# A hybrid attention block with a mixture of experts: how the overflow tables are stored, and which engine clears the row buffers

## The chip, the cores and the metric

The kernel runs on one core of one Trainium2 chip. The metric is the device time of one launch in microseconds; before the change the median of three runs is 1189.38 us (1186.39 to 1190.62).

## The reference, cut to what matters

One transformer block over 512 tokens of width 1024: three mixing branches (dilated attention, a gated recurrence, attention to a memory), gates, an output product, a layer norm, a two-level mixture of experts, a second layer norm. The change lies in the experts' part. Each token picks one of 4 groups and 2 of its 8 experts, so 1024 token-expert pairs go to 32 experts; each expert is two products (1024 to 256, twice) and one (256 to 1024):

```python
glog = (ht @ w_rg) + b_rg;  gsel = argmax(glog)
elog = ((ht @ w_re) + b_re).reshape(T, 4, 8);  top_v, top_i = top_k(elog[arange(T), gsel], 2)
weights = softmax(top_v) * gprob[gsel]
def expert_block(xb, e):
    return (silu(xb @ w_gate[e]) * (xb @ w_up[e])) @ w_down[e]
y[token] += weight * expert_block(row of token, e)          # for both picks
x = layer_norm(ALPHA * x + y)
```

## The kernel before, in words

The kernel is one long program without loops on the chip, written in Python loops. Each engine (PE, DVE, ACT, POOL, SP) has its own queue of instructions, which it works off in order; waits between engines are semaphores. The order inside a queue is made by the framework's planner from the order of the source and its own estimates, so neighbours in a queue need not be neighbours in the source.

**Before the experts.** Projections, the three branches and the output product keep PE busy up to about 850 us of the span. `norm_and_route(c)` (L660) does layer norm and routing for each of four classes of 128 tokens: the logits, the two picks (`gi`, `ei`, one-hot `oh`), the rank of each pair within its expert (`cums`, by a product with a triangle, copied by ACT at L695). `gain_and_store(c)` (L698) finishes the rows and stores them to `x1d` in DRAM.

**The experts.** Each expert has a capacity of 64 rows, and two experts make one pass `p` of 128 rows, 16 passes in all (loop at L992). The rows of a pass are `xs`. For passes 0 and 1, `gather` (L756) makes them with one-hot products on PE (L767), whose one-hot matrices `oh0` and `ohg` DVE writes in `picked` (L657). For passes 2 to 15, `fetch` (L750) gathers rows from `x1d` by an indirect DMA of POOL into one of three buffers `xg0` to `xg2`, and PE transposes them (L778). The three buffers are cleared once before the loop (L989), on POOL, as empty slots are not fetched. `gate_up` (L782, matmuls L789) makes the two first products, `silu2` the activation (L193, L194), L1010 transposes, L1023 makes the last product, and ACT and DVE scale it by the slot's weight into `y` (L1029, L1031). POOL scatters `y` by an indirect DMA to `yd` (L1037) for passes 0 to 13.

**The weights.** The experts' weights are 192 tiles of 512 KB, 12 in each pass (four `gate_up` tiles and two `down` tiles for each of two experts). `expert_raw` (L615) loads them on SP's queue (L114) into a ring of 33 buffers: a tile can be loaded when PE has used the tile 33 before it. The `gate_up` tiles of a pass come free as its L789 goes on, its `down` tiles in its L1023. After the 192 tiles SP loads `yd` back (L1046), and the second layer norm follows.

**The tables.** After `gate_up(0)` is issued, `tables` (L818) makes, for each slot, the token (`tok`, `gidx`) and the weight (`wsl`), by `slot_tables` (L793): one-hot matrices and a product (L805) into columns 0 to 15 of these [128, 24] tables. `overflow_tables` (L860) does the same for pairs beyond an expert's capacity: columns 16 to 23, eight columns of 128 slots, stored to DRAM as `ovg_d` (tokens) and `ovw_d` (weights) of 1024 numbers each (L899, L900, on POOL's queue), with a list of experts `ove_d` (L911). In DRAM slot `s` of column `p` lies at `p*128 + s`, so a column runs down the partitions on chip but is contiguous in DRAM. `overflow` (L913) reads the three in a loop at the end of the program, once for each block of 64 such rows; the profiled execution has no instruction of the loop's body (L918 on).

The scratch tiles of both functions are pieces of one buffer of the tag `yp` (L996), which has two buffers; `y` of the passes rotates through the same two (L1013), so `y` of pass 1 takes the buffer in which the scratch tiles were.

Of the kernel before, what the change touches and what calls it, by code (L numbers as in the profile page):

```python
# [13 lines left out]
I32 = mybir.dt.int32  # L14
# [22 lines left out]
def build(tc, ins, out, dbg=None):  # L37
# [5 lines left out]
    def T(pool, shape, dt=F32, tag=None, **kw):  # L43
        cnt[0] += 1
        tag = tag or f"u{cnt[0]}"
        return pool.tile(list(shape), dt, name=f"{tag}_{cnt[0]}", tag=tag, **kw)
# [23 lines left out]
    V, S, TE, G = nc.vector, nc.scalar, nc.tensor, nc.gpsimd  # L70
# [4 lines left out]
    def bank(tag, w=512, dt=F32):  # L75
        t = T(ps, [128, 512], dt, tag=tag)
        return t[:, :w] if w != 512 else t

    ident = T(cp, [128, 128], tag="ident")
# [9 lines left out]
    ovg_d = T(mdram, [1024, 1], I32, tag="ovg")  # L89
    ovw_d = T(mdram, [1024, 1], tag="ovw")  # L90
# [177 lines left out]
    with cpool:  # L268
        for h in range(4):
# [12 lines left out]
            o = bank("o")  # L282
            for c in range(4):
                cs = slice(c * 128, (c + 1) * 128)
                sc = bank("sc", 256)
# [4 lines left out]
                p = T(tp, [128, 256], tag="cp")  # L290
# [15 lines left out]
    with tc.tile_pool(name="a0", bufs=2, side="right") as tp:  # L306
# [3 lines left out]
        for j in range(5):  # L310
# [4 lines left out]
            pt = bank("sc")  # L315
# [238 lines left out]
    gidx = T(sp, [128, NPAIR], I32, tag="gidx")  # L554
    tok = T(sp, [128, NPAIR], tag="tok")
    wsl = T(sp, [128, NPAIR], tag="wsl")
    yidx = T(sp, [128, PDR], I32, tag="yidx")
    ovi = T(sp, [1, 17], I32, tag="ovi")
    lp = es.enter_context(tc.tile_pool(name="late", bufs=1))
# [13 lines left out]
    i512, i128, i64, i32, i16 = (kc[:, 0:n] for n in (512, 128, 64, 32, 16))  # L573
# [182 lines left out]
    def gather(p):  # L756

        xs = T(mp, [128, 8, 128], tag="xs")
        pts = []
        if p < PEG:  # L760
            oh_ = oh0 if p == 0 else T(mp, [128, 4, 128], tag="ohg", bufs=1)
            pts = [bank("o" if p == 0 else "tr") for _ in range(2)]
            for c in range(4):
                if p > 0:
                    picked(c, p, oh_)
                for k in range(8):
                    TE.matmul(pts[k // 4][:, k % 4 * 128:(k % 4 + 1) * 128], x1[:, c, k * 128:(k + 1) * 128],  # L767
                              oh_[:, c, :], start=c == 0 and k % 4 == 0, stop=c == 3 and k % 4 == 3)
        else:
            xg = xgs[p % AHEAD]  # L770
        for j in range(2):
            if p < PEG:
                pt = pts[j]
            else:
                pt = bank("tr")
                for k in range(4):
                    kk = j * 4 + k
                    TE.transpose(pt[:, k * 128:(k + 1) * 128], xg[:, kk * 128:(kk + 1) * 128], ident)  # L778
            (S.copy if j == 0 else V.tensor_copy)(xs[:, j * 4:(j + 1) * 4, :].rearrange("p k r -> p (k r)"), pt)
        return xs  # L780
# [12 lines left out]
    def slot_tables(lp, row, where, w3, lo, n):  # L793

        sA = T(lp, [128, 8, 128], BF, tag="sA")
        V.tensor_tensor(sA, i128[:, None, :].to_broadcast([128, 8, 128]), row.to_broadcast([128, 8, 128]),
                        op=OP.is_equal)
        sB = T(lp, [128, 8, 5, n], BF, tag="sB")
        V.tensor_scalar(sB[:, :, 0, :], where, pcol, None, op0=OP.mult)
        V.tensor_tensor(sB[:, :, 1, :], where, bval[:, :, None].to_broadcast([128, 8, n]), op=OP.mult)  # L800
        for i in range(3):
            V.tensor_tensor(sB[:, :, 2 + i, :], where, w3[:, i, :, None].to_broadcast([128, 8, n]), op=OP.mult)
        acc = bank("sc", 5 * n)
        for a in range(8):
            TE.matmul(acc, sA[:, a, :], sB[:, a, :, :].rearrange("p a b -> p (a b)"), start=a == 0, stop=a == 7)  # L805
        t = T(lp, [128, 5, n], tag="st")
        V.tensor_copy(t.rearrange("p a b -> p (a b)"), acc)
        g = slice(lo, lo + n)
        V.scalar_tensor_tensor(tok[:, g], t[:, 0, :], BIG, t[:, 1, :], op0=OP.add, op1=OP.add)
        if lo == 0:  # L810
            V.tensor_copy(yidx, tok[:, 0:PDR])
        V.tensor_scalar(t[:, 0, :], tok[:, g], 512.0, -512.0, op0=OP.is_ge, op1=OP.mult)
        V.tensor_tensor(tok[:, g], tok[:, g], t[:, 0, :], op=OP.add)
        V.tensor_copy(gidx[:, g], tok[:, g])
        V.tensor_tensor(wsl[:, g], t[:, 2, :], t[:, 3, :], op=OP.add)
        V.tensor_tensor(wsl[:, g], wsl[:, g], t[:, 4, :], op=OP.add)
# [43 lines left out]
    def overflow_tables(lp):  # L860

        oh8 = oh.rearrange("p c k e -> p (c k) e")
        t32 = T(lp, [128, 8, 32], tag="t32")
        cnt = bank("sc", 32)
        for d in range(4):
            for k in range(2):
                TE.matmul(cnt, oneb, oh[:, d, k, :], start=d == 0 and k == 0, stop=d == 3 and k == 1)
        nb7 = T(lp, [128, 32, 7], tag="nb7")
        V.tensor_tensor(nb7, cnt[:, :, None].to_broadcast([128, 32, 7]),
                        i7[:, None, :].to_broadcast([128, 32, 7]), op=OP.is_gt)  # L870
        nbl = T(lp, [128, 32], tag="nbl")
        V.tensor_reduce(nbl, nb7, axis=AX.X, op=OP.add)
        inc = T(lp, [128, 32], tag="inc")
        V.tensor_tensor_scan(inc, oneb[:, :32], nbl, 0.0, op0=OP.mult, op1=OP.add)
        exc = T(lp, [128, 32], tag="exc")
        V.tensor_tensor(exc, inc, nbl, op=OP.subtract)
        ob = T(lp, [128, 8, 1], tag="ob")
        V.tensor_tensor(t32, oh8, exc[:, None, :].to_broadcast([128, 8, 32]), op=OP.mult)
        V.tensor_reduce(ob, t32, axis=AX.X, op=OP.add)
        t7 = T(lp, [128, 8, 7], tag="t7")  # L880
        V.tensor_tensor(t7, rank8.to_broadcast([128, 8, 7]), i7[:, None, :].to_broadcast([128, 8, 7]), op=OP.is_ge)
        fl = T(lp, [128, 8, 1], tag="fl")
        V.tensor_reduce(fl, t7, axis=AX.X, op=OP.add)
        row = T(lp, [128, 8, 1], tag="row8")
        V.scalar_tensor_tensor(row, fl, -64.0, rank8, op0=OP.mult, op1=OP.add)

        blk = T(lp, [128, 8, 1], tag="blk")
        V.scalar_tensor_tensor(blk, t7[:, :, 0:1], 64.0, ob, op0=OP.mult, op1=OP.add)
        V.scalar_tensor_tensor(blk, fl, -65.0, blk, op0=OP.add, op1=OP.add)
        oh16 = T(lp, [128, 8, 16], tag="oh16")  # L890
        V.tensor_tensor(oh16, i16[:, None, :].to_broadcast([128, 8, 16]), blk.to_broadcast([128, 8, 16]), op=OP.is_equal)
        ohp = oh16.rearrange("p a (b w) -> p a b w", w=2)
        pair = T(lp, [128, 8, 8], tag="pair")
        V.tensor_reduce(pair, ohp, axis=AX.X, op=OP.add)
        par = T(lp, [128, 8, 1], tag="par8")
        V.tensor_reduce(par, ohp[:, :, :, 1], axis=AX.X, op=OP.add)
        V.scalar_tensor_tensor(row, par, 64.0, row, op0=OP.mult, op1=OP.add)
        slot_tables(lp, row, pair, w3, 16, 8)
        G.dma_start(ovg_d.rearrange("(p s) o -> s (p o)", s=128), gidx[:, 16:])  # L899
        G.dma_start(ovw_d.rearrange("(p s) o -> s (p o)", s=128), wsl[:, 16:])  # L900
        z1, z2 = (T(lp, [1, 16, 32], BF, tag=t) for t in ("sA", "t32"))
        ib = i128[0:1, 0:16, None].to_broadcast([1, 16, 32])
        V.tensor_tensor(z1, ib, exc[0:1, None, :].to_broadcast([1, 16, 32]), op=OP.is_ge)
        V.tensor_tensor(z2, ib, inc[0:1, None, :].to_broadcast([1, 16, 32]), op=OP.is_lt)
        V.tensor_tensor(z1, z1, z2, op=OP.mult)
        V.tensor_tensor(z1, z1, i32[0:1, None, :].to_broadcast([1, 16, 32]), op=OP.mult)
        ovf = T(lp, [1, 16], tag="ovf")
        V.tensor_reduce(ovf, z1, axis=AX.X, op=OP.add)
        V.tensor_copy(ovi[:, 0:16], ovf)
        V.tensor_copy(ovi[:, 16:17], inc[0:1, 31:32])  # L910
        G.dma_start(ove_d.rearrange("a o -> o a"), ovi[:, 0:16])  # L911
# [74 lines left out]
    xgs = []  # L986
    for j in range(AHEAD):
        xgs.append(T(mp, [128, 1024], tag=f"xg{j}", bufs=1))
        G.memset(xgs[j], 0.0)  # L989
    xs = gather(0)  # L990
    group = []
    for p in range(16):  # L992
        expert_raw(12 * p + 12 + len(ring))
        gu = gate_up(p, xs)
        if p == 0:
            part = Parts(T(mp, [128, 2048], tag="yp"))  # L996
            tables(part)
            overflow_tables(part)
            for j in range(1, AHEAD + 1):
                fetch(j)  # L1000
# [7 lines left out]
        pt = bank("tr", 256)  # L1008
# [185 lines left out]
```

## Time and profile before

| what | value |
|---|---|
| median of three runs | 1189.38 us |
| profiled execution, its own time | 1191.01 us |
| its span in the trace | 1189.1 us |
| PE busy | 1111.0 us (93%) |
| DVE busy | 504.1 us (42%) |
| ACT busy | 442.9 us (37%) |
| POOL busy | 84.7 us (7%) |
| moved by DMA | 200.91 MB, mean 169 GB/s |

The span is what the trace covers, and the execution's own time is 1.9 us longer. Busy shares are means over stages with different limits: the mean rate of 169 GB/s hides stages with 400 GB/s. Times such as "908" are us from the span's start.

### The profile page before, as it was taken

What the parts mean: (1) busy time and instruction counts of PE and PEld (TensorE: products, weight loads), DVE (VectorE), ACT (ScalarE), POOL (GpSimd) and SP (SyncE); (2) the same over time, 40 slices, a digit from 0 to 9 for tenths busy, and PEclk for the clock granted to TensorE, in tenths of its full rate; (3) what the DMA queues carried; (4) which work ended last, traced back from release to release, by engine and by line L of the source; (5) the groups of instructions that cost most, each with busy time, mean ns of one, the idle gap of its engine ahead of it and who ended that gap; (6) DMA issues with size and microseconds to landing.
All of it is one profiled execution on the core that took longest, in us unless ns stands there. A gap on an engine that the chain in (4) does not pass through costs nothing.

```text
span 1189.1 us, 17191 instructions
## 1 busy us (share of the span) xinstructions
PE 1111.0 (93%) x6830; PEld 779.2 (66%) x6830; DVE 504.1 (42%) x998; ACT 442.9 (37%) x762; POOL 84.7 (7%) x104
## 2 busy tenths in 40 slices
PE   6999999999999999999999999999989988888872
PEld 4788677777777887887887877888774333223231
DVE  4544387776676323323224223336574111111145
ACT  6965467665655433233233333225011111101112
POOL 1000130000000000000000000000323111110003
PEclk9999999999999999999999999999999999999986
DMA  8633241222222632322331333335659999999961
GB/s 295 217 94 88 91 130 54 64 81 64 80 63 80 185 105 62 93 89 66 98 97 49 93 91 130 121 100 214 262 195 240 314 408 405 402 403 399 410 254 71
DMA packets 69650, 200.91 MB, mean 169 GB/s; under 512 B 16719, under 2 KB 18843, under 8 KB 69568
## 3 DMA queue, kind: packets, MB, share of 16 engines
q1 hardware_dynamic: 62640, 183.92, 45.6%
q0 software_dynamic: 6928, 15.87, 4.1%
q8 instruction: 55, 0.90, 0.3%
q14 instruction: 27, 0.22, 0.1%
HBM read 191.23 MB, written 17.81 MB: 176 GB/s over the span
## 4 chain that ended last, share of the span: by engine, by line
PE 76%; DMA 13%; ACT 4%; DVE 3%; issue 2%; SPq 0%; ACTq 0%; POOL 0%; DVEq 0%; POOLq 0%
PE pj L131 49%; DMA raw<-in_wexp_dram 11%; PE pj L789 5%; PE tr L217 3%; PE o L1023 3%; PE pj L718 2%; PE o L718 2%; DMA raw<-in_w_in_dram 1%; PE sc L357 1%; PE sc L511 1%; DMA wh<-in_wexp_dram 1%; PE o L533 1%; ACT bvt L338 1%; PE o L299 1%; PE o L530 1%
## 5 line engine op out<-in xcount | busy, mean ns | idle before, releaser
L84 DVE TENSOR_TENSOR wl<-raw,wh 128x1024 fp32r<-128x1024 f32 (+1 forms) x129 | 148.1, 1149 | 268.3 <-PE pj L131 179.1
L83 ACT CAST wh<-raw 128x1024 fp32r<-128x1024 f32 (+1 forms) x137 | 132.3, 967 | 247.9 <-PE pj L131 237.5
L131 PE MATMUL pj<-xh,wh 128*128 128x512 f32 x760 | 204.5, 401 | 5.1 <-ACT wh L83 5.1
L131 PE MATMUL pj<-xl,wh 128*128 128x512 f32 x760 | 199.8, 397 | 0.0
L131 PE MATMUL pj<-xh,wl 128*128 128x512 f32 x760 | 194.1, 394 | 0.0
L131 PEld LDWEIGHTS pj<-xh,wl 128*128 128x128 f32 x760 | 141.8, 188 | 32.5 <-issue 2.1
L131 PEld LDWEIGHTS pj<-xh,wh 128*128 128x128 f32 x760 | 139.8, 189 | 35.1 <-ACT wh L83 6.4
L131 PEld LDWEIGHTS pj<-xl,wh 128*128 128x128 f32 x760 | 140.7, 188 | 29.7 <-issue 0.9
L789 PE MATMUL pj<-raw,xs 128*64 128x512 f32 x432 | 125.2, 605 | 13.0 <-DMA raw<-in_wexp_dram 12.1
L789 PEld LDWEIGHTS pj<-raw,xs 128*64 128x64 f32 x432 | 36.0, 137 | 82.3 <-issue 49.3
L193 ACT ACTIVATE esg<-pj 128x256 f32<-128x256 f32 x16 | 6.1, 384 | 134.8 <-PE pj L789 134.8
L194 DVE SCALAR_TENSOR_TENSOR esg<-esg,pj 128x256 f32<-128x256 f32 x16 | 6.7, 421 | 116.8 <-ACT esg L193 116.8
L1023 PE MATMUL o<-raw,ehT 128*64 128x512 f32 x204 | 52.5, 604 | 1.2 <-ACT ehT L1011 0.5
L1031 DVE TENSOR_SCALAR yp<-o,wsl 128x512 f32<-128x512 f32 x14 | 10.5, 750 | 69.9 <-PE o L1023 69.8
L388 ACT ACTIVATE bx<-bx 128x512 f32<-128x512 f32 x48 | 30.4, 633 | 19.3 <-DVE bx L387 18.7
L1023 PEld LDWEIGHTS o<-raw,ehT 128*64 128x64 f32 x204 | 16.6, 140 | 28.6 <-issue 24.0
L131 PE MATMUL pj<-oh,wh 128*128 128x512 f32 x128 | 34.9, 400 | 0.0
L131 PE MATMUL pj<-oh,wl 128*128 128x512 f32 x128 | 34.3, 395 | 0.0
L131 PE MATMUL pj<-ol,wh 128*128 128x512 f32 x128 | 33.2, 391 | 0.0
L209 DVE SCALAR_TENSOR_TENSOR sg<-sg,pj 128x512 f32<-128x512 f32 x16 | 11.0, 686 | 40.2 <-PE pj L131 40.2
L131 PEld LDWEIGHTS pj<-ol,wh 128*128 128x128 f32 x128 | 24.0, 188 | 5.3
L131 PEld LDWEIGHTS pj<-oh,wl 128*128 128x128 f32 x128 | 23.9, 188 | 5.2
(377 smaller groups left out, 1448.1 us busy)
## 6 DMA issues: line engine op xcount, KB each, us to landing
raw<-in_wexp_dram SPq DMA_DIRECT2D x159, 512.0 KB, 11.1
raw<-in_w_in_dram SPq DMA_DIRECT2D x95, 512.0 KB, 3.6
wh<-in_wexp_dram SPq DMA_DIRECT2D x18, 512.0 KB, 11.3
wl<-in_wexp_dram SPq DMA_DIRECT2D x15, 512.0 KB, 11.3
yd<-merged SPq DMA_DIRECT2D x8, 512.0 KB, 6.3
raw<-in_w_kv_dram SPq DMA_DIRECT2D x8, 512.0 KB, 3.7
raw<-in_w_bb_dram SPq DMA_DIRECT2D x8, 512.0 KB, 3.6
raw<-in_w_out_dram SPq DMA_DIRECT2D x8, 512.0 KB, 3.8
```

Of the source, the lines that this page charges most:

```text
L83: S.copy(h, src)
L84: (eng or V).tensor_tensor(l, src, h.bitcast(F32), op=OP.subtract)
L131: TE.matmul(acc, wt[:, k * 128:(k + 1) * 128], m[:, k, :], start=n == 0, stop=n == 3 * kt - 1)
L217: TE.transpose(pt[:, j * 128:(j + 1) * 128], src[:, j * 128:(j + 1) * 128], ident)
L299: TE.matmul(o[:, cs], v[:, js], pT[:, js], start=j == 0, stop=j == 1)
L338: S.copy(nat(vT), cls(acc))
L357: TE.matmul(sc[g * 32:(g + 1) * 32, j * w:(j + 1) * w].rearrange("p (a t) -> p a t", t=32), keys[:, gs], queries[:, :, gs], start=True, st ...
L388: S.activation(X, X, AF.Exp)
L511: TE.matmul(s1[g * 32:(g + 1) * 32, :], qs[0][:, c * 128 + g * 32:c * 128 + (g + 1) * 32], ks[0][:, lows[g] * 128:lows[g] * 128 + 256], st ...
L718: TE.matmul(acc, m[:, k, cs], w[:, j * 512:(j + 1) * 512], start=k == 0 and n == 0, stop=k == 7 and n == 2)
L789: TE.matmul(acc[rows_, :], xs[:, j * 2 + k, rows_], raws[2 * p + q, j][:, k * 512:(k + 1) * 512], start=j == 0 and k == 0, stop=j == 3 and ...
L1023: TE.matmul(acc[rows_, :], hT[:, k * 128 + q * 64:k * 128 + (q + 1) * 64], raws[2 * p + q, 4 + k][:, n * 512:(n + 1) * 512], start=k == 0, ...
```

## The change

Two edits. The two stores of the overflow tables are replaced: PE transposes columns 16 to 23 of `tok` and of `wsl` into one PSUM bank ([8, 128] each), DVE copies the one into `ovq` (with the conversion to integers), ACT the other into `ovv` (both in scratch pieces of the buffer `yp`), and POOL stores the two from 8 partitions with 512 contiguous bytes each. What lies in DRAM afterwards is the same. And the three row buffers `xg` are cleared by ACT, in six halves of 128x512 (`i512` times zero), not by POOL.

```diff
@@ overflow_tables @@
         slot_tables(lp, row, pair, w3, 16, 8)
-        G.dma_start(ovg_d.rearrange("(p s) o -> s (p o)", s=128), gidx[:, 16:])
-        G.dma_start(ovw_d.rearrange("(p s) o -> s (p o)", s=128), wsl[:, 16:])
+        pt = bank("sc", 256)
+        TE.transpose(pt[:8, 0:128], tok[:, 16:24], ident)
+        TE.transpose(pt[:8, 128:256], wsl[:, 16:24], ident)
+        ovq = T(lp, [8, 128], I32, tag="nb7")
+        V.tensor_copy(ovq, pt[:8, 0:128])
+        ovv = T(lp, [8, 128], tag="sB")
+        S.copy(ovv, pt[:8, 128:256])
+        G.dma_start(ovg_d.rearrange("(p s) o -> p (s o)", s=128), ovq)
+        G.dma_start(ovw_d.rearrange("(p s) o -> p (s o)", s=128), ovv)
@@ before the loop over the passes @@
         xgs.append(T(mp, [128, 1024], tag=f"xg{j}", bufs=1))
-        G.memset(xgs[j], 0.0)
+        for h in range(2):
+            S.mul(xgs[j][:, h * 512:(h + 1) * 512], i512, 0.0)
```

## Rows read from the trace of the kernel before

**Rows 1.** The page, the span in 40 equal slices: what DMA moved.
```profile
GB/s 295 217 94 88 91 130 54 64 81 64 80 63 80 185 105 62 93 89 66 98 97 49 93 91 130 121 100 214 262 195 240 314 408 405 402 403 399 410 254 71
```
**Rows 2.** The chain that ended last, from 700 us: start us, us, what.
```profile
918.87 3.43 PE o L1023 x16
...
932.07 3.43 PE o L1023 x16
...
965.14 12.05 DMA raw<-in_wexp_dram
...
1125.28 10.18 DMA wh<-in_wexp_dram
```
**Rows 3.** Windows: stretch, us; busy us of PE, PEld, DVE, ACT, POOL; PEclk, DMA share, GB/s.
```profile
904.00:908.00 4.00, 4.00 (x24) 1.35 (x22) 3.31 (x12) 0.69 (x1) 0.84 (x2) 1.00 0.62 190
908.00:912.00 4.00, 4.00 (x22) 1.58 (x20) 1.04 (x5) 0.00 (x0) 2.94 (x4) 1.00 0.86 289
912.00:920.00 8.00, 7.71 (x36) 2.84 (x34) 1.44 (x3) 1.35 (x3) 1.38 (x2) 1.00 1.43 92
920.00:924.00 4.00, 4.00 (x22) 1.42 (x20) 0.75 (x1) 0.69 (x1) 0.00 (x0) 1.00 0.98 306
924.00:932.00 8.00, 7.71 (x38) 2.82 (x34) 1.45 (x3) 1.35 (x3) 2.05 (x2) 1.00 1.03 101
932.00:936.00 4.00, 4.00 (x22) 1.34 (x20) 0.42 (x1) 0.69 (x1) 0.00 (x0) 1.00 0.96 338
936.00:964.00 28.00, 27.44 (x126) 9.72 (x124) 4.72 (x9) 4.08 (x8) 4.55 (x5) 1.00 1.03 410
```
**Rows 4.** Timeline of POOL: start us, us, instruction [idle before, and its releaser].
```profile
880.46 2.75 POOL L989 MEMSET xg<- 128x1024 f32 x3
...
907.78 0.99 POOL L900 DMA_DIRECT2D ovw<-wsl  x1 [3.16 <-DVE wsl L816]
...
910.86 0.94 POOL L899 DMA_DIRECT2D ovg<-gidx  x1
```
**Rows 5.** DMA issues: out<-in, queue, count, KB each, median us from issue to landing.
```profile
raw<-in_wexp_dram SPq DMA_DIRECT2D x159, 512.0 KB, 11.1
...
yd<-yp,yidx POOLq DMA_INDIRECT x14, 7.4
...
ovw<-wsl POOLq DMA_DIRECT2D x1, 4.0 KB, 13.2
ovg<-gidx POOLq DMA_DIRECT2D x1, 4.0 KB, 20.6
```
**Rows 6.** Timeline of SP, 900 to 912 us.
```profile
906.59 5.43 SPq L114 DMA_DIRECT2D raw<-in_wexp_dram  x8
```
**Rows 7.** Timeline of DVE, 868 to 912 us.
```profile
879.76 0.32 DVE L657 TENSOR_SCALAR ohg<-kc,cums,memb 128x64 f32<-128x64 f32 x1
...
880.06 3.20 DVE L657 TENSOR_SCALAR ohg<-kc,cums,memb 128x64 f32<-128x64 f32 x1
...
885.60 0.53 DVE L657 TENSOR_SCALAR oh<-kc,cums,memb 128x64 f32<-128x64 f32 x2
```
**Rows 8.** Timeline of PE, 876 to 892 us.
```profile
878.66 2.65 PE L767 MATMUL o<-oh,x 128*128 128x128 f32 x22
883.37 0.91 PE L767 MATMUL tr<-ohg,x 128*128 128x128 f32 x6 [2.06 <-issue]
...
887.37 2.07 PE L767 MATMUL o<-oh,x 128*128 128x128 f32 x16
```
**Rows 9.** Timeline of ACT: the last class's logits and ranks, and the output of pass 1.
```profile
883.38 0.16 ACT L682 COPY lg<-sc 128x4 f32<-128x4 f32 x1 [6.86 <-DVE ohg L657]
...
885.23 0.17 ACT L695 COPY cums<-sc 128x32 f32<-128x32 f32 x1
...
920.66 0.69 ACT L1029 ACTIVATE yp<-o,wsl 128x512 f32<-128x512 f32 x1 [2.38 <-PE o L1023]
```
**Rows 10.** Groups by line on ACT: a multiplication by a constant, 128x512 (count, busy us, mean ns).
```profile
L604 ACT ACTIVATE xh<-merged 128x512 fp32r<-128x512 f32 x8 | 4.6, 622 | 1.2 <-DVE merged L211 1.2
```

## The prediction

> **What bounds the kernel now.** I begin with the page's slices [rows 1]: in slices 33 to 38, some 180 us, DMA moves about 400 GB/s without a break, and nowhere else. The reader should see a stage that lives on DMA's rate, with a broken start before it (214, 262, 195, 240 and 314 GB/s). The chain that ended last [rows 2] says the same by name: PE's passes follow each other every 13.20 us (918.87 to 932.07) until 965, and from there to 1135.5 the chain is weights that land. A pass takes 12 weight tiles, one gather and one scatter of 0.5 MB each, 14 x 0.524 = 7.3 MB; at the 410 GB/s of 936 to 964 [rows 3] that is 17.9 us, against 13.2 us of PE. So from the first passes on DMA is the slower one, PE lives on the 33 tiles loaded ahead until 965, and the end of the kernel is set by when the last of 192 tiles lands. A microsecond in which DMA could load and doesn't is lost for good.
>
> Next the windows around the tables [rows 3]. In 904 to 908 DMA is partly idle (share 0.62, 190 GB/s): the ring is full, and SP goes on at 906.59 with eight loads as PE gives up pass 0's last tiles [rows 6]. That ends there. In 912 to 920 and 924 to 932 it is otherwise: a share of 1.43 and 1.03, so engines at work, but 92 and 101 GB/s moved. Two holes with a better stretch between them (306). Then I looked at what POOL issued [rows 4]: the store of the weights' table at 907.78, that of the tokens' table at 910.86. They take 13.2 and 20.6 us to land [rows 5], so they end at 921.0 and 931.5, where the first and the second hole end. Both store columns, 1024 separate numbers each.
>
> **Part one: the stores.** Removed: 2 x 1024 pieces of 4 B. Added: 2 x 8 rows of 512 B. What the holes cost: in 908 to 936 the five rows moved 4x289 + 8x92 + 4x306 + 8x101 + 4x338 = 5276 kB, where 28 us at 410 make 11480. Lacking are 6.2 MB, 15.1 us at 410 [rows 3]. That is the upper end. The lower end counts only the two holes: 16 us at a mean of 96.5 instead of 410, 16 x (410 - 96.5)/410 = 12.2 us. In 908 to 912 the loads have just restarted, which stays. I take 14.5, near the upper end, since the holes' edges (932 to 936, 920 to 924) are theirs too.
>
> Can DMA use the time, or would the ring stop it? Pass 0's last tiles are free from 906.59 on [rows 6]; pass 1's gate-up tiles follow two by two until its L1023 begins, the last two about 919; its down tiles at 921 to 922.3, as that L1023 begins at 918.87 and lasts 3.43 [rows 2]. DMA needs 1.28 us a tile (0.524 MB at 410): from 906.6 ten tiles and two indirect transfers take it to about 922, and the last four tiles of pass 1 to 927. It is always a little behind PE, by 2 us at first and by 17.9 - 13.2 = 4.7 us more in each pass. So the ring stays out of the way, if only just in pass 1; I keep 2 us of loss there for the range. Nor does PE become the bound: from 932.07 + 3.43 = 935.5 (end of pass 2) thirteen passes of 13.2 us end at 1107, while the tiles, at 1135.5 before, still end near 1120. PE only runs dry later than at 965.
>
> The trace shows a page's rule tested. 1024 numbers of 4 B take 10 us or more and leave 92 to 101 GB/s for the rest [rows 3 to 5]. The Trainium skill ("DMA: Bandwidth & Descriptors", section "Bandwidth", the table measured for loads) gives 0.68 us for 4 KB, as 64 packets an engine of about 10.5 ns. By that, an estimate, two tables would cost 1.4 us of DMA and this term would be 1.4 instead of 14.5; the trace does not agree, unless the holes have another cause.
>
> New work: two transposes on PE, a copy on DVE, one on ACT, each below the 0.69 us of a 128x512 copy [rows 9], and two POOL issues shorter than or equal to the 0.99 and 0.94 us they replace [rows 4]. I cost these at nothing. What hides them is PE's lead over DMA in pass 1; if the transposes stood in PE's queue before the second half of L1023 of pass 0, PE would wait for the tables and the tiles would come free up to 3 us late. Behind POOL's stores wait the scatter of pass 0 and later gathers, which get faster. One new wait: the stores now read a scratch piece of the `yp` buffer that `y` of pass 1 takes at 920.66 [rows 9]. Issued near 910 and landing like a scatter (7.4) [rows 5], they are done by 918. If they were as late as 931.5, ACT and DVE would stand 11 us in pass 1, and esg of pass 2 behind them.
>
> **Part two: the clears.** POOL's three clears run 880.46 to 883.21 [rows 4]. In the same time DVE's second pick, begun at 880.06, takes 3.20 us, where the first took 0.32 [rows 7], and ends with POOL's work. Behind it stand the last class's second pick, its rank and its one-hot (885.60), and PE: L767 of classes 0 to 2 ends at 881.3, then PE idles 2.06 us for `ohg` [rows 8]. Without the stall `ohg` is there at 881.3; the products of 883.37 to 887.37, some 4 us, start 2.06 us sooner; the last class's at 887.37 follow, if their one-hot is ready. So 2.1 us is the upper end, and pass 0 starts, tiles come free and the full DMA stretch begins that much earlier. Against it ACT has six clears of 128x512, by the nearest row 0.622 us each [rows 10], 3.7 us. If they stand in ACT's queue ahead of the ranks' copy at 885.23 [rows 9], the one-hot is no earlier than before; PE has then done `ohg` already and gains about 1 us or nothing; at worst the copy of `cums` or of `xs` comes late and pass 0 starts up to 3.7 us later. Ends: 2.1 gained, 3.7 lost. ACT is idle for the 6.86 us before the last class's logits at 883.38 [rows 9], room for all six if their buffers are free by then, so I take 1.5 gained, nearer to that end.
>
> **Sum.** 1191.0 (the profiled execution; its span of 1189.1 and 1.9 around it) - 14.5 - 1.5 = 1175.0. That execution is 1.6 us above the median of 1189.4, so against the median 1173.4.
>
> **Rivals.** First, *the ring stops it*: PE loses some us in pass 1 or 0 (the wait for the `yp` buffer, the transposes early in PE's queue), tiles come free late and DMA idles in front of a full ring for 6 to 8 of the us won. For it: the lead is only 2 us there. Against: it grows by 4.7 us a pass. About 1181.
>
> Second, *the holes aren't the stores'*, or the new stores are still written in small pieces: POOL's queue also holds the scatter of pass 0 and gathers in that time. Against: 936 to 964 holds such transfers in every pass at 410 GB/s [rows 3], and both holes end as a table lands. Then only part two is left: 1189.4 - 1.5 = 1188. The Trainium skill's 10.5 ns a packet would be this case, with 1.4 us more.
>
> Third, *slower*: the six clears on ACT stand ahead of the ranks' copy or of the first `xs` copy; pass 0 begins up to 3.7 us later, and DMA, idle before it, with it: 1189.4 + 3.7 = 1193. It decides only where the stores give back less than 3.7 us. For it: the queue's order isn't shown. Against: the holes' price.
>
> **Numbers.** A measurement of this kernel can tell about 0.3%, 3.6 us, from no change. Forecast (gain of 10 to 19 us) 0.83; the ring 0.06; the holes not the stores' 0.07; slower 0.04. Faster 0.89, same 0.07, slower 0.04. The likeliest case reaches from 15.1 + 2.1 = 17.2 gained (1172), with 4 us of scatter of the runs, to 12.2 gained less 2 of the ring (1179). I take 1168 to 1182, which holds the first rival's 1181; the two others, with 0.11, lie outside.
>
> **What would show it.** Right: after the change no stretch between 908 and 936 below 350 GB/s with a share near 1; the stores land in under 10 us; DMA at 400 or more from about 906 on; PE dry not at 965 but around 1020 to 1040; the last weight tile about 16 us earlier; no pick of DVE over 1 us near 880, and L767 before pass 0 done at 887.3 to 888.5 instead of 889.4. Wrong: holes that stay with stores that land early; `y` of pass 1 waiting for a DMA; SP waiting for PE in passes 1 to 4; ACT's clears between the last class's logits and its ranks.

## The result, and the profile after

The changed kernel takes 1170.65 us (median of four runs, 1169.99 to 1170.94), the kernel before 1187.89 in the same comparison (four runs, 1185.76 to 1190.62): a ratio of 0.9856, interval 0.9836 to 0.9875, so 17.2 us less. I had forecast 1173.4, within 1168 to 1182. The profiled execution takes 1169.99 us, its span is 1167.8.

Three marks cut a span into parts that can be compared: the last class's FIND_INDEX8 on DVE (`gi`, L676), the first L789 on PE, and SP's first load of `yd`, which follows the last weight tile.

| us | start to `gi` | `gi` to first L789 | first L789 to first `yd` load | from there to the end |
|---|---|---|---|---|
| before | 879.61 | 9.76 | 242.33 | 57.40 |
| after | 877.24 | 5.96 | 228.86 | 55.74 |
| gained | 2.37 | 3.80 | 13.47 | 1.66 |

The four gains add up to 21.3 us, the difference of these two profiled spans; the medians differ by 17.2. The first part holds nothing that the change touches: over the twelve profiles of all kernels here `gi` lies between 877.24 and 879.73, and in the second profiles of before and after (below) at 878.50 and 878.27, so I take its 2.4 us for chance. The third is the weights' stream with the holes, the second the clears.

The page's slices of the changed kernel, what DMA moved:

```profile
GB/s 300 221 103 81 93 133 55 64 80 67 65 82 78 163 120 67 90 90 68 90 91 55 91 96 49 203 99 108 384 207 227 401 407 405 400 398 405 406 269 73
```

The full stretch is one slice longer than in [rows 1] (32 to 38). The windows of the changed kernel (columns as in [rows 3]):

```profile
900.00:904.00 4.00, 4.00 (x18) 1.37 (x18) 3.44 (x13) 0.00 (x0) 0.00 (x0) 1.00 0.78 222
904.00:908.00 4.00, 4.00 (x19) 1.29 (x19) 0.28 (x1) 0.25 (x1) 2.65 (x4) 1.00 0.93 302
908.00:912.00 4.00, 3.71 (x18) 1.53 (x17) 1.44 (x3) 1.01 (x3) 1.07 (x1) 1.00 1.02 406
912.00:920.00 8.00, 8.00 (x38) 2.63 (x38) 0.75 (x1) 1.03 (x2) 1.04 (x1) 1.00 1.03 411
920.00:924.00 4.00, 3.76 (x19) 1.61 (x16) 1.15 (x3) 0.97 (x2) 0.33 (x1) 1.00 1.03 411
924.00:932.00 8.00, 8.00 (x38) 2.63 (x38) 1.04 (x2) 1.07 (x2) 1.57 (x2) 1.00 1.03 407
```

Where [rows 3] had 92 and 101 GB/s stand 411 and 407. What is left of loss lies at 900 to 908, with shares below 1: there the ring is full. What filled the engines in the holes shows when the queues are told apart, in 908 to 936 us, first before and then after (q1 is the queue of SP's loads, q0 POOL's; packets, MB, and the time that the packets took as a share of 16 engines' span):

```profile
q1 hardware_dynamic: 1258, 4.60, 95.4%
q0 software_dynamic: 503, 0.68, 15.0%
```

```profile
q1 hardware_dynamic: 2856, 10.40, 92.5%
q0 software_dynamic: 713, 1.03, 10.0%
```

The loads' packets were under way for the same share of the time in both, but before they moved less than half as much: a packet of q1 took 28 us x 16 x 0.954 / 1258 = 0.34 us, after the change 0.145. So the holes are loads that go on slowly. They are not engines taken up by the tables' pieces, which are only a part of q0's 15.0%. POOL's queue, where [rows 4] had the two column stores and the clears:

```profile
877.55 0.57 POOL L704 DMA_DIRECT2D x1d<-x  x1 [8.20 <-DVE gi L676]
893.55 1.23 POOL L752 DMA_INDIRECT xg<-x1d,gidx  x1 [15.43 <-DVE yp L878]
...
905.34 0.58 POOL L906 DMA_DIRECT2D ovg<-yp  x1 [0.24 <-issue]
905.92 0.53 POOL L907 DMA_DIRECT2D ovw<-yp  x1
```

The clears are gone between the first two lines, and the stores take 0.58 and 0.53 us of POOL. DVE's second pick, which took 3.20 us in [rows 7], in its timeline:

```profile
877.69 0.31 DVE L657 TENSOR_SCALAR ohg<-kc,cums,memb 128x64 f32<-128x64 f32 x1
```

It takes 0.31 us. The clears now stand in ACT's timeline:

```profile
877.48 1.15 ACT L997 ACTIVATE xg<-kc 128x512 f32<-128x512 f32 x2 [3.34 <-DVE gi L676]
878.54 0.14 ACT L682 COPY lg<-sc 128x4 f32<-128x4 f32 x1
878.58 1.15 ACT L997 ACTIVATE xg<-kc 128x512 f32<-128x512 f32 x2
879.64 0.17 ACT L695 COPY cums<-sc 128x32 f32<-128x32 f32 x1
...
880.87 1.28 ACT L822 ACT_TABLE_LOAD   x1
```

They do stand about the last class's logits and ranks, as I feared, but two at a time, so that each copy finds a place. And one thing is new: the ranks' copy (L695) comes ahead of the table load of the next function (1.28 us). Before it came behind it, at 885.23 [rows 9]. The chain that ended last (columns as in [rows 2]):

```profile
912.93 3.43 PE o L1031 x16
926.08 3.43 PE o L1031 x16
...
1022.11 12.43 DMA raw<-in_wexp_dram
```

The passes keep 13.2 us, and PE runs dry at 1022, not at 965.

### The profile page after: what moved, and what is told of

Its sections match the earlier page's. It is cut to its first block, busy times and chain, and to the rows that moved or that the text cites. A ratio compares the mean times of both kernels' runs of the same rounds, so it can differ in the third digit from the quotient of the medians.

```text
span 1167.8 us, 17200 instructions
## 1 busy us (share of the span) xinstructions
PE 1100.6 (94%) x6832; PEld 776.2 (66%) x6832; DVE 501.6 (43%) x999; ACT 446.1 (38%) x769; POOL 79.9 (7%) x101
## 4 chain that ended last, share of the span: by engine, by line
PE 83%; DMA 7%; ACT 4%; DVE 3%; issue 2%; SPq 0%; ACTq 0%; POOL 0%; DVEq 0%; POOLq 0%
PE pj L131 50%; PE pj L789 8%; DMA raw<-in_wexp_dram 5%; PE o L1031 4%; PE tr L217 3%; PE o L718 2%; PE pj L718 2%; PE sc L357 1%; PE sc L511 1%; DMA raw<-in_w_in_dram 1%; PE o L533 1%; ACT bvt L338 1%; PE o L299 1%; PE o L530 1%; PE sc L673 1%
## 5 line engine op out<-in xcount | busy, mean ns | idle before, releaser
L789 PE MATMUL pj<-raw,xs 128*64 128x512 f32 x432 | 118.6, 598 | 5.9 <-DMA raw<-in_wexp_dram 4.8
L789 PEld LDWEIGHTS pj<-raw,xs 128*64 128x64 f32 x432 | 34.9, 136 | 69.6 <-issue 48.3
L1031 PE MATMUL o<-raw,ehT 128*64 128x512 f32 x204 | 53.3, 617 | 1.5 <-ACT ehT L1019 0.9
L1039 DVE TENSOR_SCALAR yp<-o,wsl 128x512 f32<-128x512 f32 x14 | 10.5, 749 | 65.2 <-PE o L1031 65.2
L1031 PEld LDWEIGHTS o<-raw,ehT 128*64 128x64 f32 x204 | 16.6, 139 | 28.3 <-issue 23.5
```

Source lines behind the costliest of these rows:

```text
L789: TE.matmul(acc[rows_, :], xs[:, j * 2 + k, rows_], raws[2 * p + q, j][:, k * 512:(k + 1) * 512], start=j == 0 and k == 0, stop=j == 3 and ...
L1031: TE.matmul(acc[rows_, :], hT[:, k * 128 + q * 64:k * 128 + (q + 1) * 64], raws[2 * p + q, 4 + k][:, n * 512:(n + 1) * 512], start=k == 0, ...
```

## The experiments

**The parts apart.** One kernel has only the stores by rows, one only the clears on ACT: the change's diff, one hunk each.

> The stores by rows, POOL still clears. My theory (the two parts are separate): no hole between 904 and 936 (every 4 us at 290 GB/s or more), the last pass's L1031 (the down products) ends 240 to 242 us after the first L789, as with both parts (240.8) and not 255.9 as before; but the first L789 comes 9 to 10 us after the last class's FIND_INDEX8 (gi, L676), as before (9.8), not 6.0. Time 14 to 16 us below before, about 1173. Rival (the gain hangs on the clears, which start the experts earlier and shift the stores): less than 8 us, about 1180 or more.

Measured: 1174.46 us, ratio 0.9894 (0.9879 to 0.9910), 12.2 us below the 1186.64 of before; `gi` to first L789 8.55 (I had expected 9 to 10), the stream 227.99 us, the end of the last down products 241.53 after the first L789, as expected. DMA in the windows around the tables:

```profile
900.00:904.00 4.00, 4.00 (x23) 1.47 (x24) 3.31 (x10) 0.38 (x1) 2.03 (x1) 1.00 0.86 321
904.00:908.00 4.00, 4.00 (x20) 1.27 (x18) 2.75 (x12) 0.69 (x1) 0.63 (x1) 1.00 0.64 211
908.00:912.00 4.00, 4.00 (x20) 1.29 (x17) 0.13 (x1) 0.25 (x1) 2.02 (x4) 1.00 0.91 342
```

The holes are gone with the clears still on POOL; what stays is the ring's wait at 904 to 908, below the 290 GB/s that I had expected. The gain is 2 to 4 us smaller than I wrote, so my size for the stores was too large.

> ACT clears, the stores piece by piece as before. My theory: the two holes stay (some 16 us at about 100 GB/s), first L789 to the end of the last down products 255 to 257 us; the first L789 6 to 7 us after the last class's gi, so 2 to 4 us below before, about 1184. Rival one (the clears are hidden in the end, DMA being the bound anyway): within 1 us of before. Rival two (ACT's 3.5 us stand in the route's way): slower by 1 to 3 us.

Measured: 1182.14 us, ratio 0.9962 (0.9947 to 0.9977), 4.5 us below before; `gi` to first L789 5.97, the stream 238.49, to the end of the last down products 250.35, short of the 255 that I expected. Its holes, in the windows:

```profile
912.00:916.00 4.00, 4.00 (x18) 1.26 (x18) 0.21 (x1) 0.49 (x2) 0.65 (x1) 1.00 0.88 60
916.00:920.00 4.00, 4.00 (x22) 1.40 (x20) 0.75 (x1) 0.58 (x1) 0.00 (x0) 1.00 1.03 180
920.00:924.00 4.00, 4.00 (x21) 1.47 (x18) 0.06 (x1) 0.38 (x1) 0.00 (x0) 1.00 0.93 144
```

The parts add up: 1.06% and 0.38% apart, 1.44% together. Neither rival holds: the clears count though DMA sets the end, since the stream begins with the first pass.

**Is it the pieces, and how many?** Three kernels, all with the clears on ACT.

```diff
 # one_table: the weights by rows, the tokens as before
+G.dma_start(ovg_d.rearrange("(p s) o -> s (p o)", s=128), gidx[:, 16:])
+G.dma_start(ovw_d.rearrange("(p s) o -> p (s o)", s=128), ovv)
 # act_queue: both as before, from ACT's queue
+S.dma_start(ovg_d.rearrange("(p s) o -> s (p o)", s=128), gidx[:, 16:])
+S.dma_start(ovw_d.rearrange("(p s) o -> s (p o)", s=128), wsl[:, 16:])
 # pieces_32: no transposes, slot by slot in DRAM
+G.dma_start(ovg_d.rearrange("(s p) o -> s (p o)", s=128), gidx[:, 16:])
+G.dma_start(ovw_d.rearrange("(s p) o -> s (p o)", s=128), wsl[:, 16:])
```

> ACT clears, the weights' table by rows, the tokens' table still as 1024 pieces. My theory (each table's pieces fill DMA for some 7.5 us): one hole of 7 to 9 us at about 100 GB/s after its issue, time 7 to 8 us above the changed kernel, about 1178. Rival (one table alone is hidden behind the indirect transfers, the hole needs both): under 2 us above the changed kernel.

Measured: 1178.42 us, ratio 0.9936 (0.9917 to 0.9956), 7.8 us above the changed kernel's 1170.65; the stream 234.32. One hole, in the windows:

```profile
912.00:916.00 4.00, 4.00 (x18) 1.26 (x18) 0.31 (x1) 0.39 (x2) 0.74 (x1) 1.00 0.96 55
916.00:920.00 4.00, 4.00 (x22) 1.31 (x20) 0.75 (x1) 0.68 (x1) 0.00 (x0) 1.00 0.97 184
920.00:924.00 4.00, 4.00 (x20) 1.47 (x17) 0.00 (x0) 0.38 (x1) 1.00 (x1) 1.00 1.00 381
```

One table costs about half of two. The stream gives 234.32 - 228.2 (the mean of two profiles of the changed kernel) = 6.1 us for 1024 pieces, and 238.49 - 228.2 = 10.3 for the 2048 with the clears alone.

> ACT clears, both tables as 2 x 1024 pieces as before, but issued on ACT's queue and not on POOL's. My theory (the pieces themselves fill the DMA engines, whoever issues them): the holes stay, 12 to 16 us lost, about 1184, within 3 us of the kernel with the clears alone. Rival (it is POOL's queue and its descriptors, which the indirect scatter and gathers wait behind): no holes, within 3 us of the changed kernel, about 1171.

Measured: 1181.22 us, ratio 0.9951 (0.9936 to 0.9967), with the clears alone 1182.14; the stream 239.14. So the holes don't need POOL's queue. But two different things make them here:

```profile
912.00:916.00 4.00, 4.00 (x18) 1.26 (x18) 0.37 (x1) 0.38 (x1) 0.79 (x1) 1.00 0.96 230
916.00:920.00 4.00, 4.00 (x20) 1.29 (x18) 0.75 (x1) 0.69 (x1) 0.75 (x1) 1.00 0.89 211
920.00:924.00 4.00, 4.00 (x20) 1.42 (x17) 0.00 (x0) 0.32 (x1) 0.26 (x1) 1.00 0.56 84
924.00:928.00 4.00, 3.71 (x19) 1.44 (x18) 1.44 (x3) 1.03 (x3) 1.03 (x1) 1.00 0.25 46
```

Up to 920 the loads that are under way go on at about half their rate, with the engines busy, as they do beside POOL's stores. After that most of the 16 engines are idle, and SP's queue says why. Its timeline from 907.6 us (two loads in 17.54 us: one at 907.75, the next at 924.97), and its longest wait in 908 to 936 (us in total, times, longest):

```profile
907.75 17.54 SPq L114 DMA_DIRECT2D raw<-in_wexp_dram  x2
```

```profile
SPq L114 <- DMA ovw<-wsl: 16.8, 1, 16.8
```

SP waited for the weights' table to land. In this trace SP's loads use eight completion semaphores in turn, each load waits for the transfer that used its semaphore last, and the two stores from ACT's queue took two of the eight. POOL's stores use others. So this kernel loses a part of its time by a wait that the others don't have; that 239.14 comes out so near to 238.49 is in part chance, and it is not shown that a table costs the same whoever issues it.

It shows something else, as each piece is here a packet of its own (ACT's queue, 908 to 936 us, columns as above):

```profile
q10 hardware_dynamic: 2079, 0.01, 4.2%
```

28 us x 16 x 0.042 / 2079 = 9 ns a piece: by their own time the two tables take 1.2 us of the engines, not 10. My theory, that the pieces themselves fill the engines, is wrong in its words. Why the loads' packets take longer beside them the traces don't show.

> ACT clears; no transposes: each table is stored as 128 pieces of 32 B, one from each partition, in another order in DRAM (slot by slot instead of column by column; the loop over the overflow, which runs no times here, would have to read it so). My theory (a table costs DMA time by its number of pieces, 1024 before): an eighth of the loss, under 1.5 us above the changed kernel, no stretch of 4 us after 908 under 350 GB/s; about 1171. Rival (any store in pieces below 512 B stalls the engines): half the holes or more stay, 1177 or more.

Measured: 1172.56 us, ratio 0.9882 (0.9866 to 0.9899). By the medians that is 1.9 us above the changed kernel, more than expected; but the stream is 227.36, none of it in the weights' stage, and the last part is 58.0 us where the changed kernel has 55.7, which I take for chance (at the end of this section). The issues (columns as in [rows 5]):

```profile
ovw<-wsl POOLq DMA_DIRECT2D x1, 4.0 KB, 6.0
ovg<-gidx POOLq DMA_DIRECT2D x1, 4.0 KB, 6.6
```

and the windows:

```profile
908.00:912.00 4.00, 3.71 (x16) 1.46 (x13) 1.43 (x3) 0.97 (x2) 0.61 (x1) 1.00 1.02 390
912.00:920.00 8.00, 8.00 (x38) 2.69 (x38) 0.77 (x2) 1.07 (x2) 1.48 (x2) 1.00 1.03 407
```

No hole with 256 pieces of 32 B, where 2048 of 4 B made two. The rival, that every small piece stalls the engines, falls, and POOL's queue by itself makes no hole. Whether the number of the pieces counts or their size is not told apart, as both changed by eight: by number alone 256 pieces would cost 6.1 x 256 / 1024 = 1.5 us, and two profiles of the changed kernel differ by 1.4. The loop over the overflow runs no times with these inputs; it would have to be written for this order.

**DVE's stall.** The stores by rows, and POOL clears each buffer twice.

```diff
         G.memset(xgs[j], 0.0)
+        G.memset(xgs[j], 0.0)
```

> The stores by rows; POOL clears each of the three row buffers twice. My theory (DVE stands still as long as POOL clears, and the first pass waits for DVE): one DVE operation near the last class's gi (L676) lasts about 6 us and not 3.2, the first L789 comes 11 to 13 us after gi where it was 8.6 with single clears, and the time is 2 to 4 us above the kernel with the stores alone, about 1178. Rival (the gain of the clears on ACT came from another order of ACT's work, not from DVE's stall): first L789 8 to 9 us after gi, time as with the stores alone.

Measured: 1176.56 us, ratio 0.9920 (0.9902 to 0.9938): 2.1 us above the kernel with the stores alone by medians, 3.1 by the ratios; `gi` to first L789 12.38. The pick in DVE's timeline:

```profile
878.72 4.99 DVE L657 TENSOR_SCALAR ohg<-kc,cums,memb 128x64 f32<-128x64 f32 x1
```

5.0 and not 6, as it came through between two of the clears; the first pass was as late as expected, for a second reason, in the windows (the column before the last two is the granted clock of TensorE):

```profile
880.00:884.00 4.00, 0.19 (x1) 0.22 (x2) 3.94 (x4) 0.16 (x1) 3.94 (x6) 0.84 0.25 99
884.00:888.00 4.00, 4.00 (x20) 3.94 (x21) 3.94 (x24) 1.68 (x4) 0.67 (x1) 0.50 0.00 0
```

PE was all but idle in the first (0.19 of 4 us), and then at 0.50, the lower of its two levels (1.2 of 2.4 GHz). So the stall is the cause, and PE pays for it once more after it. The first pass comes 3.8 us later than with single clears and the time grows by less, as the last part of the span is 2.3 us shorter (55.7 beside 58.0), again by chance as I take it.

**Second profiles.** The kernels before and after, unchanged.

> The kernel before once more, for a second profile. My theory now (the holes' length varies from run to run, and the first profile had long ones, as its time of 1191.0 lay above the median): first L789 to the end of the last down products 250 to 255 us, not 255.9; the time 1185 to 1190. Rival (the holes are always 15 us): 255 to 257 us again.

Measured: 1184.77 us, 0.2 below what I gave; to the end of the last down products 251.42, the stream 239.57, `gi` to first L789 8.55. The holes do vary: 242.33 in the profile I predicted from, 239.57 here.

> The changed kernel once more, for a second profile and a time beside the next kernel's. My theory: 1170 to 1173 us, a ratio to before of 0.984 to 0.989; first L789 5.9 to 6.1 us after the last class's gi, and 240 to 242 us from there to the end of the last down products; no stretch of 4 us between 908 and 936 under 380 GB/s. Rival (the first profile was a lucky one and the gain is nearer to the 14.5 us of stores and clears apart): 1174 or more.

Measured: 1169.50 us, 0.5 below what I gave, ratio 0.9859 (0.9831 to 0.9887); 5.96 and 227.50, to the last down products 239.37, a little under the 240 that I gave. The pair of second profiles gains 2.59 before the first L789 and 12.07 in the stream.

**Is more to be had at 900 to 908?** Two kernels move the one-hot gather of pass 1, which lies on PE between pass 0's two products, so that pass 0's down tiles come free later than DMA wants them.

```diff
 # gather_late: all of it behind pass 0's down products
-        if p < 15:
+        if 0 < p < 15:
             xs = gather(p + 1)
...
+        if p == 0:
+            xs = gather(p + 1)
+            fetch(p + 1 + AHEAD)
 # gather_split: classes 0 and 1 ahead of them, 2 and 3 behind
+        if p == 0:
+            half = first_half()
...
+        if p == 0:
+            xs = gather(1, half)
```

> The changed kernel with the one-hot gather of pass 1 put behind pass 0's last products in the source, so that pass 0 starts sooner and its down tiles come free some 5 us earlier. My theory (what DMA still loses lies where the ring is full, before the first tile comes free and at 900 to 908): 2 to 4 us below the changed kernel, about 1167. Rival (the end is no longer set by these stretches): within 1 us of the changed kernel, 1170 to 1171.

Measured: 1174.43 us, ratio 0.9893 (0.9877 to 0.9910), slower than the changed kernel; the stream 230.80. Both theories missed: the wait has moved to pass 1's first tiles, as the windows show:

```profile
904.00:908.00 4.00, 4.00 (x35) 3.55 (x35) 1.01 (x5) 0.84 (x2) 1.62 (x3) 1.00 0.85 312
908.00:912.00 4.00, 4.00 (x20) 1.30 (x18) 0.13 (x1) 0.00 (x0) 0.00 (x0) 1.00 0.33 108
```

SP's longest wait from 896 to 918 is for pass 1's L789 (7.1 us). PE lost time too: it stood 2.3 us ahead of pass 0's down products, and its granted clock was 0.71 in 896 to 900, where the changed kernel has 1.00.

> The changed kernel with the one-hot gather of pass 1 cut in two in the source: classes 0 and 1 ahead of pass 0's down products, classes 2 and 3 behind them. My theory (DMA idles where the ring waits for pass 0's down tiles, and, with the whole gather behind them, for pass 1's first tiles; a cut between gives the tiles in time for both): 1 to 2.5 us below the changed kernel. Rival (PE's total work before pass 1 is what counts, or the planner moves it all again): within 1 us of it, or up to 4 us above as with the whole gather behind.

Measured: 1168.88 us, ratio 0.9845 (0.9819 to 0.9872), beside 1169.50 of the changed kernel on the same chip: no difference that can be told. In the windows it does what it should:

```profile
904.00:908.00 4.00, 4.00 (x20) 1.29 (x20) 1.22 (x5) 0.25 (x1) 1.63 (x3) 1.00 0.99 347
908.00:912.00 4.00, 4.00 (x20) 1.57 (x16) 0.53 (x2) 0.72 (x2) 0.00 (x0) 1.00 1.03 409
```

and its stream is 226.20, 1.3 us less; but its last part is 57.90 where the changed kernel has 55.77. That part differs by its clock, in windows of the kernel with the stores alone (57.99):

```profile
1124.00:1128.00 4.00, 4.00 (x14) 1.27 (x11) 0.00 (x0) 0.00 (x0) 0.00 (x0) 0.59 1.02 410
...
1132.00:1136.00 4.00, 3.01 (x5) 1.78 (x6) 3.97 (x4) 0.00 (x0) 0.00 (x0) 0.50 0.13 54
```

and of the changed kernel's second profile (55.77):

```profile
1124.00:1128.00 4.00, 0.00 (x0) 0.00 (x0) 3.61 (x5) 2.22 (x3) 0.00 (x0) 1.00 0.95 380
1128.00:1132.00 4.00, 3.88 (x7) 1.98 (x7) 3.93 (x5) 0.00 (x0) 0.00 (x0) 0.58 0.20 79
```

After the last weights PE's work is on the path, and it makes a difference of some 2 us whether the lower level falls on the last down products and the sums behind them or on the sums alone. The kernels that end with 57 to 58 us are not of one kind (the first profile of before is one, the second isn't), so I take it for chance and not for an effect of an edit.

## Why the prediction was right, and where it wasn't

**The bound.** The end is set by the weights' stream, and a microsecond that DMA loses there comes back as one at the end: shown by the parts apart and by one table. That PE would become no bound and only run dry later, I had at 1020 to 1040; it is 1022.

**The stores.** The holes are the stores', as I had it: by rows they are gone, with one table in columns about half is left, and with pieces of 32 B on the same queue there are none. What a piece does I had only as "engines at work"; it was the loads' own packets that kept the engines at work, 0.34 us each instead of 0.145. The pieces, where the trace shows them singly, take 9 ns. Why the packets take longer stays open. The size was off: 14.5 us in the sum, 12.2 by the medians of the kernel with the stores alone, which is the lower end of the bounds that I gave (12.2 to 15.1). The step that failed is "In 908 to 912 the loads have just restarted, which stays. I take 14.5, near the upper end". Two things are wrong in it. It reckons from one profile, and that one had long holes: 242.33 in the stream, in the second 239.57; against the 227.99 of the stores alone that is 14.3 and 11.6. And it sets DMA free at 410 GB/s from 908 on, where the ring's wait does not end with the holes: the kernel with the stores alone has 211 and 342 GB/s in 904 to 912, (2x410 - 211 - 342) x 4/410 = 2.6 us of loss, the changed kernel at 900 to 908 (2x410 - 222 - 302) x 4/410 = 2.9. So the rival of the ring held, for a small part.

**The page's rule.** The Trainium skill ("DMA: Bandwidth & Descriptors", "Bandwidth") gives about 10.5 ns a packet, measured for loads. For the pieces' own time the trace agrees, with 9 ns each from ACT's queue. As the price of the store it is far too low: one table takes 6.1 us from the loads, 95 ns for each of the 64 pieces that an engine has of it on average. I wrote "the trace does not agree, unless the holes have another cause": they have, and it is not the packets' own time.

**The clears.** 1.5 us in the sum, 2.1 as upper end; measured 4.5 alone, 3.8 on top of the stores (1174.46 - 1170.65). The step that failed is "So 2.1 us is the upper end". It counts the 2.06 us that PE idles behind DVE's stall [rows 8] and nothing else. From `gi` to the first L789 the two kernels without a fall of TensorE's clock there, the one with the stores alone and the changed one, differ by 8.55 - 5.96 = 2.59. Of that 2.06 is the wait for `ohg`, and 0.34 a second wait of PE for DVE, for the last class's one-hot, which stands behind the stall too, here with the stores alone:

```profile
883.37 0.20 PE L692 MATMUL sc<-oh,trib 128*128 128x32 bf16 x2 [0.34 <-DVE oh L687]
```

The 0.2 that is left I can't place. In the profile I predicted from the same part took 9.76, 1.2 more. There PE lost its clock behind the idle time, which I had the rows to see and hadn't looked at. The window of the kernel before:

```profile
884.00:888.00 4.00, 3.66 (x22) 3.48 (x21) 3.96 (x27) 1.49 (x4) 0.00 (x0) 0.57 0.00 0
```

The granted clock is 0.57, toward the lower of its two levels, and the twelve products for `ohg` that run there take 2.91 us in PE's timeline, in the kernel with the stores alone 1.58. The second profile of before and the kernel with the stores alone have the same 2.06 us of idle time and 1.00 in that window. So in all three profiles the stall costs PE the 2.06 us, and in one of them 1.2 more. The whole part from `gi` to the first L789 makes 2.6 to 3.8 us of the 3.8 to 4.5; the rest the profiles don't place: it is within the scatter of the start (`gi` at 877.24 to 879.73 over twelve profiles) and of the tail.

On ACT the clears cost 1.15 for two, 0.58 each, against the 0.622 of [rows 10]. They took the very place that I had listed as a wrong sign, between the last class's logits and its ranks, and it cost nothing: they come two at a time, and the copy of `cums` stands at 879.64, right behind the second pair. Rival three named the right place and the wrong price.

**The sum.** The stores were 2.3 us too large (14.5 for 12.2), the clears 2.3 to 3.0 too small (1.5 for 3.8 to 4.5). The two errors cancel, which is why 16.0 stands so near to 17.2. The total is not evidence for either term; only the kernels with one part each showed them.

**What I costed at nothing.** The transposes take 0.27 us each, at 904.35 and 904.46 in PE's timeline. They lie among pass 1's L789, in the stretch in which the ring is full. Whether they cost a part of the loss at 900 to 908 was not tried by itself; the kernel without transposes and with 32 B pieces has the same stream (227.36 beside 227.50). The wait for the scratch piece of `yp` did not occur: ACT's first write of pass 1's output waits for PE's product and for nothing else,

```profile
914.78 0.69 ACT L1037 ACTIVATE yp<-o,wsl 128x512 f32<-128x512 f32 x1 [2.44 <-PE o L1031]
```

**The other signs.** In 908 to 936 no stretch of 4 us is below 403 GB/s. The first load of `yd`, right behind the last weight tile's, issues at 1112.06 instead of 1131.70, 19.6 us earlier, of which 2.4 are the earlier `gi`; for the last tile I had about 16. The second pick is 0.31. L767 before pass 0 is done at 883.2, not at 887.3 to 888.5: 2.4 us are the earlier `gi` again, the rest is the clears, worth more than I had. The new stores land in 6.9 and 6.6 us in the second profile. One sign of being wrong did come: SP waits 4.2 us for pass 1's L1031, up to 915.5. It cost nothing that shows, as the loads already issued kept DMA at 406 GB/s and more in 908 to 916.

## What to carry to other kernels

Count the pieces of a store, not its bytes: 4 KB in 1024 pieces of 4 B took 6.1 us from the whole core's loads, and the same 4 KB in 128 pieces of 32 B took none that could be seen, so a layout of longer pieces is worth a pair of transposes. The price is not in the store's own time on the engines but in the transfers beside it. When a transfer is moved to another queue to test this, look at what the other queues then wait for: here a semaphore in common held the loads for 16.8 us. Where DMA sets the end, whatever delays the first release of a full ring counts too, even on engines that are idle most of the time. Take marks in two or three profiles of the same kernel before sizing a term: here one profile's longer holes made one term some 2 us too large, and the other lacked 1.2 us that the same profile's lower clock had cost.

## What the runs showed of the hardware that I had not expected

A DVE instruction can stand for as long as POOL clears: 3.20 us behind three clears, 4.99 behind five of six, 0.31 without them. What runs beside it decides, not its own 64 elements a partition.

Pieces of 4 B slow other traffic far beyond their own time: 9 ns each where they are seen singly, from ACT's queue, and in the kernel before the loads' packets around them took 0.34 us instead of 0.145. The cause stays open.

The same 2.06 us without work on PE were followed once by a granted clock of 0.57 and twice by 1.00; after 0.19 us busy in 4 it was 0.50.
